# A two-layer decoder step: two small transfers change their queues, and the decode queries are spread in one step instead of two

## The chip, the cores and the metric

The kernel runs on one core of a Trainium2 chip. A core has TensorE (PE in the rows; PEld is its weight load), VectorE (DVE), ScalarE (ACT), GpSimd (POOL) and SyncE (SP), each with its own in-order stream of instructions, and 16 DMA engines that serve the queues on which SP, ACT and POOL issue transfers. The metric is the device time of one execution in microseconds (us).

## The reference

One inference step of a two-layer decoder for two groups with shared weights: a prompt of 512 tokens, and 8 samples of 8 new tokens each, which have 1024 tokens of past (576 token columns in all, model width 1024, float32). In short:

```
h = rmsnorm(x, norm1);  q, k, v, u, ga, gb = split(h @ w_in)        # 12 heads of 64
q, k = rope(q), rope(k)                                             # first 16 of 64 features
for (w, d) in ((128, 1), (512, 4), (2048, 16)):                     # 4 heads each
    query t attends keys t, t-d, t-2d, ... (w // d + 1 of them), in prompt or cache + new
o_a = the three groups' outputs mixed by softmax of their log-sum-exps
o_b = (mean of the last 2, 4, 8, 16 rows of u, minus u) @ pool_lin * pool_scale
x  = x + (sigmoid(ga) * (o_a @ w_pa) + sigmoid(gb) * (o_b @ w_pb)) @ w_o
x  = x + square(relu(rmsnorm(x, norm2) @ w_up)) @ w_down
outputs: final rmsnorm of x, the updated key/value windows of prompt and samples,
         the last 15 rows of u of the prompt (poolp) and of each sample (pools)
```

## The kernel before

Activations are kept transposed: features on partitions, the 576 tokens along the row. Every large product is done in three matmuls (high parts, and each low part with the other's high part); each weight tile is loaded by SP into `raw` or `rawu`, its high part is cast by ACT (`wh`) and its low part made by DVE (`wl`).

A layer goes through these stages. First q, k, v: for two head pairs p = 0, 1, units "d", "a", "b", "e", "c" (`qkv`, e for p = 0 alone), in which tokens stand on partitions; `unit_out` scales the result into `nat` (ACT; two buffers) and the samples' part into `DN`. While these run, the prompt's attention (`prompt(p)`) and the samples' attention (`decode(p, qb)`) of pairs 0 and 1 are woven in. Then the four `u` products of the pooling branch (`u_out`, `windows`, `lin`), the gate products with `w_pb` and `w_pa`, the `w_o` product, and the MLP, in which the sample caches are copied to the outputs from POOL's queue.

The order is written out at build time. PE's stream drives a clock `now`; generators ("sides") are resumed when that clock, a lane's modelled time or a marked event allows it. `Lane` and `Matrix` (lines 329 to 384) are models of the engines, and `transfer` (line 362) is that of a DMA: when the issuing engine has issued it and when it will have landed. They decide only where an instruction stands in its engine's stream; on the chip semaphores decide when it runs.

What the change touches:

- `turn(p, nat)`: values of unit c are needed with token 4n + r on partition n. `nat` (512 KB) is written to `DV` in HBM and read back as `vc` in that order, both on SP. `prompt(p)` uses `vc` in the matmuls into `O`. The `out_p` stores of `unit_out` read the same `nat`, also from SP.
- When pair 1's scores are done, the pool that holds `nat` is closed, and the tiles `u0` to `u3` are allocated in its memory (`pool_open`), so the first write to `u` waits for whoever still reads `nat`.
- `decode_q(p, DN)`: the 64 rows of queries (8 samples b, 8 tokens t, 384 numbers each) must stand in `qb` as 128 partitions (b, g), g = 0 to 15, each with all 8 tokens of its sample. They are stored to `DQ` (96 KB), spread to `DR` in HBM (1536 KB, 16 copies per sample), and loaded as `qb`. Pair 1 waits for event "K" of pair 0 ahead of the load, since `qb` has one buffer. `decode` multiplies cached keys (`kc`, four buffers, loaded by SP) with `qb` on DVE and POOL.
- `windows(sn)`: the last rows of u are transposed into PSUM (`pot`, one buffer), copied to `pn` by ACT, and stored: one store for `poolp`, eight for `pools`. `pn` is a tile of tag "t" with three buffers, which the gates' tiles (`tb`) and others use too. `lin` takes its PSUM from the same buffer as `pot`.

Of the kernel before, what the change touches and what calls it, by code (L numbers as in the profile page):

```python
# [7 lines left out]
F32 = mybir.dt.float32  # L8
# [9 lines left out]
NT, NP = 576, 512  # L18
NK = D // 128
UL = 15 + NP + 8 * 23  # L20
# [71 lines left out]
def hybrid_decoder_kernel(ctx: ExitStack, tc: tile.TileContext, a, o):  # L92
    nc = tc.nc
    T, V, S, G, Q = nc.tensor, nc.vector, nc.scalar, nc.gpsimd, nc.sync
# [4 lines left out]
    tp = ctx.enter_context(tc.tile_pool(name="tmp", bufs=3))  # L99
# [5 lines left out]
    drp = ctx.enter_context(tc.tile_pool(name="dr", bufs=1, space=DRAM))  # L105
# [12 lines left out]
    def v3(v, n):  # L118
        return v.rearrange("p (n d) -> p n d", n=n)
# [124 lines left out]
    def side(gen, delay=0.0):  # L244
        sides.append([now[0] + delay if not isinstance(delay, tuple) else delay, gen])

    def mark(*key, lat=0.0):
        ev[key] = now[0] + lat
# [27 lines left out]
    def place(x):  # L276

        t = x.tensor
        key = seen.get(t.name)
        if key is None:  # L280
            k = (t.slot_key, t.tag) if getattr(t, "slot_key", None) is not None else (t.name, None)
            n = count[k] = count.get(k, -1) + 1
            key = seen[t.name] = (k, n % (getattr(t, "bufs", None) or 1))
            old = slots.get(key)
            slots[key] = [max([old[0]] + [e[4] for e in old[1] + old[2]]) if old else 0.0, [], []]
        (step, n), *rest = x.ap
        p0, lo = divmod(x.offset, step) if step else (0, x.offset)
        return key, (p0, p0 + n, lo, lo + sum((c - 1) * abs(d) for d, c in rest) + 1)
# [4 lines left out]
    def hits(es, a, me):  # L293
        return [e[4] + (0.0 if e[5] is me else 0.1) for e in es
                if e[0] < a[1] and a[0] < e[1] and e[2] < a[3] and a[2] < e[3]]

    def due(outs, ins, me):
        t = 0.0
        for x in ins:
            key, a = place(x)  # L300
            t = max([t] + hits(slots[key][1], a, me))
        for x in outs:
            key, a = place(x)
            t = max([t, slots[key][0]] + hits(slots[key][1], a, me) + hits(slots[key][2], a, me))
        return t

    def note(outs, ins, end, me):
        for xs_, w in ((outs, 1), (ins, 2)):
            for x in xs_:
                key, a = place(x)  # L310
                es = slots[key][w]
                es[:] = [e for e in es if not (a[0] <= e[0] and e[1] <= a[1] and a[2] <= e[2] and e[3] <= a[3]
                                               and e[4] <= end)][-60:]
                es.append((*a, end, me))
# [8 lines left out]
    def size(x):  # L323
        n = 1
        for d in x.shape[1:]:
            n *= d
        return n
# [32 lines left out]
    wire, port = [0.0], [0.0]  # L360

    def transfer(lane, outs, ins):
        lane.t = max(lane.t, due(outs, ins, None)) + (0.5 if lane is G else 0.06)
        n = 4e-3 * outs[0].shape[0] * size(outs[0])
        wire[0] = max(wire[0], lane.t) + n / 270.0
        note(outs, ins, wire[0] + 1.9, wire)

    class Matrix:
# [26 lines left out]
    def ready(*aps, lag=0.2):  # L395
        return "at", max(now[0], due([], aps, None)) + lag
# [3 lines left out]
    S = Lane(S, 0.19, 1190.0)  # L400
    G = Lane(G, 0.12, 440.0)
    Q = Lane(Q, 0.0, 1.0)
# [102 lines left out]
    def rope(x, cos, sin, P, n, h):  # L505
        c16 = cos.unsqueeze(2).to_broadcast([P, n, h, 16])
        s16 = sin.unsqueeze(2).to_broadcast([P, n, h, 16])
        ta = tp.tile([128, 2, 256], F32, tag="t", name="rope")
        A = ta[:P, 0, :n * h * 16].rearrange("p (n h d) -> p n h d", n=n, h=h)
        B = ta[:P, 1, :n * h * 16].rearrange("p (n h d) -> p n h d", n=n, h=h)  # L510
        x16 = x[:, :, :, 0:16]
        V.tensor_mul(A, x16, c16)
        V.tensor_mul(B, x16, s16)
        V.tensor_add(x[:, :, :, 0:8], A[:, :, :, 0:8], B[:, :, :, 8:16])
        V.tensor_add(x[:, :, :, 8:16], A[:, :, :, 8:16], B[:, :, :, 0:8])
# [30 lines left out]
    for l in range(L):  # L546
# [80 lines left out]
        oa, tts, dns, vcs = [None, None], [{}, {}], [None, None], [None, None]  # L627
# [95 lines left out]

        def turn(p, nat):
            DV = drp.tile([512, 256], F32, tag=f"dv{l}{p}", name="DV")
            Q.dma_start(DV.rearrange("(j p) f -> p j f", j=4), nat)
            yield 2.8
            if p:
                yield ("O", 0)
            vcs[p] = pp.tile([128, 4, 256], F32, tag="vc", name="vc", bufs=1)  # L730
            Q.dma_start(vcs[p], DV.rearrange("(n r) f -> n r f", r=4))
            mark("V", "c", p, lat=3.0)

        def prompt(p):
# [127 lines left out]
        def decode_q(p, DN):  # L862
            rope(DN[:, 0:6].rearrange("p n (h d) -> p (n h) d", h=2).unsqueeze(1), *rope_d, 64, 1, 12)
            yield 1.6
            DQ = drp.tile([64, 384], F32, tag=f"dq{l}{p}", name="DQ")
            Q.dma_start(DQ, DN[:, 0:3].rearrange("p n f -> p (n f)"))
            yield 2.6
            DR = drp.tile([128, 3072], F32, tag=f"dr{l}{p}", name="DR")
            Q.dma_start(DR.rearrange("(b g) e -> b g e", b=8),
                        DQ.rearrange("(b t) e -> b (t e)", b=8).unsqueeze(1).to_broadcast([8, 16, 3072]))  # L870
            yield 3.6
            if p == 1:
                yield ("K", 0)
            qb = dp.tile([128, 8, 3, 128], F32, tag="qb", name="qb", bufs=1)
            Q.dma_start(qb.rearrange("p t n f -> p (t n f)"), DR)
            side(decode(p, qb))

        def decode_new(p, DN):
# [188 lines left out]
        up = bp = None  # L1067
# [19 lines left out]
        def windows(sn):  # L1087
            yield 3.0
            yield ready(sn, lag=1.0)
            ptr = trp.tile([128, 512], F32, tag="tr", name="trs")  # L1090
            for g in range(4):
                T.transpose(ptr[:, 120 * g:120 * g + 120], sn[:, 128 * g:128 * g + 128], ident[0:120, 0:120])
            for g in range(4):
                S.copy(v3(U[g][:, 15 + NP:], 8)[:, :, 0:15], v3(ptr[:, 120 * g:120 * g + 120], 8))
            for g in (3, 2, 1, 0):
                yield ("u", g, l)
                cur = U[g]
                for d in range(g + 1):
                    w = 1 << d
                    nx = up.tile([128, UL], F32, tag="s", name="s", bufs=2)  # L1100
                    s0 = 2 * w - 1
                    V.tensor_add(nx[:, s0:], cur[:, s0:], cur[:, s0 - w:UL - w])
                    cur = nx
                    yield after(V, lag=0.0)
                V.tensor_mul(cur[:, 15:31], cur[:, 15:31], cnt[:, g])
                if g == 0:
                    yield ("ob", 3, l)
                pg = up.tile([128, NT], F32, tag="pg", name="pg", bufs=3)
                sc = 1.0 / (2 << g)
                V.scalar_tensor_tensor(out=pg[:, 0:NP], in0=cur[:, 15:15 + NP], scalar=sc, in1=U[g][:, 15:15 + NP],  # L1110
                                       op0=ALU.mult, op1=ALU.subtract)
                V.scalar_tensor_tensor(out=v3(pg[:, NP:], 8), in0=v3(cur[:, 15 + NP:], 8)[:, :, 15:23], scalar=sc,
                                       in1=v3(U[g][:, 15 + NP:], 8)[:, :, 15:23], op0=ALU.mult, op1=ALU.subtract)
                pgs[g] = pg
                mark("pg", g, l, lat=max(V.t - now[0], 0.0))
                yield after(V, lag=0.0)
            for n in range(2):
                pot = trp.tile([128, 512], F32, tag="tr", name="trp")
                m = 15 if n == 0 else 64
                for g in range(4):  # L1120
                    src = U[g][:, NP:NP + 15] if n == 0 else ud[:, g]
                    T.transpose(pot[0:m, 128 * g:128 * g + 128], src, ident)
                pn = tp.tile([128, NT], F32, tag="t", name="pn")
                S.copy(pn[0:m, 0:512], pot[0:m, :])
                if n == 0:
                    Q.dma_start(o["poolp"][l], pn[0:15, 0:512])
                else:
                    for b in range(8):
                        Q.dma_start(o["pools"][l, b, 7:15], pn[8 * b:8 * b + 8, 0:512])
                yield 1.0  # L1130
            mark("w", l)

# [73 lines left out]
        for f in range(8):  # L1206
# [9 lines left out]
            t = gate.pop(0)  # L1216
# [411 lines left out]
```

## Time and profile before

| | us |
|---|---|
| median of 3 runs | 1762.05 (1757.75 to 1764.63) |
| profiled execution | 1757.92 |
| its span, first to last instruction | 1756.2 |
| PE busy | 1632.0 |
| DVE busy | 1158.4 |
| ACT busy | 695.4 |
| POOL busy | 229.7 |
| mean granted clock of TensorE | 0.962 of full speed |

The DMA engines moved 255.21 MB, a mean of 145 GB/s; SP's queue carried 198.46 MB of it. An engine that is idle costs time only where PE, the busiest, waits for it in turn. The rows of the trace are read with that question: at which places does PE stand, and what ends its wait.

### The profile page before, as it was taken

The numbers are of one execution on the slowest core, as the hardware profiler recorded it, in microseconds if no ns is written. First come the engines' busy times: TensorE is split into PE (matmuls) and PEld (weight loads), VectorE is DVE, ScalarE is ACT, GpSimd is POOL, SyncE is SP. The second block draws the span as 40 slices with busy tenths as digits, with TensorE's granted clock in tenths as the row PEclk, the third lists the DMA queues.
The fourth block names the chain that finished last, engine by engine and source line by source line (L and its number), as shares of the span: only waits on it lengthen the run. The fifth ranks groups of instructions, "written<-read, shape, count | busy, mean of one in ns | idle before, by whom it ended". The sixth has DMA issues, their size and how long they took to land.

```text
span 1756.2 us, 30640 instructions
## 1 busy us (share of the span) xinstructions
PE 1632.0 (93%) x12608; PEld 1585.7 (90%) x12608; DVE 1158.4 (66%) x1892; ACT 695.4 (40%) x1210; POOL 229.7 (13%) x350
## 2 busy tenths in 40 slices
PE   8989778899989999999999889798998999999995
PEld 8989768889889999999999878697997999999995
DVE  5589468745766666666736865884566776666763
ACT  6545232123444433344445433221344433344443
POOL 0041013000011111121001400230000211111202
PEclk9999889989989999999999999898998999999998
DMA  4564543434235545552427364325251445554521
GB/s 172 182 191 151 176 124 108 135 97 134 101 114 190 184 163 179 191 174 86 138 77 253 118 220 148 112 88 141 88 189 44 173 169 172 191 177 162 180 64 54
DMA packets 140005, 255.21 MB, mean 145 GB/s; under 512 B 9660, under 2 KB 100284, under 8 KB 137034
## 3 DMA queue, kind: packets, MB, share of 16 engines
q1 hardware_dynamic: 135498, 198.46, 35.4%
q0 software_dynamic: 3648, 53.98, 8.5%
q8 instruction: 99, 1.62, 0.4%
q10 hardware_dynamic: 720, 0.82, 0.1%
q14 instruction: 40, 0.33, 0.1%
HBM read 239.40 MB, written 74.87 MB: 179 GB/s over the span
## 4 chain that ended last, share of the span: by engine, by line
PE 78%; DVE 9%; DMA 6%; ACT 4%; issue 2%; SPq 1%; POOL 1%; POOLq 0%; DVEq 0%; ACTq 0%
PE mm L380 42%; PE mmq L380 10%; PE pa L380 10%; PE pc L380 5%; PE pb L380 2%; DVE wl L357 2%; DMA DV<-nat 2%; PE po L380 2%; PE psd L380 2%; DMA kc<-in_c 1%; ACT wh L357 1%; SPq L340 1%; PE sp L380 1%; PE O L380 1%; DVE SC L357 1%
## 5 line engine op out<-in xcount | busy, mean ns | idle before, releaser
L380 PE MATMUL mm<-m,wh 128*128 128x256 f32 (+1 forms) x2560 | 451.6, 297 | 3.4 <-DVE xr L357 2.1
L380 PEld LDWEIGHTS mm<-m,wh 128*128 128x128 f32 x2560 | 387.6, 190 | 4.4 <-ACT wh L357 1.7
L380 PE MATMUL mm<-m,wl 128*128 128x320 f32 (+1 forms) x1280 | 282.3, 298 | 7.2 <-DVE wl L357 7.2
L357 DVE TENSOR_TENSOR wl<-raw,wh 128x1024 fp32r<-128x1024 f32 (+2 forms) x195 | 218.5, 1122 | 83.4 <-ACT wh L357 80.1
L357 ACT CAST wh<-rawu 128x512 fp32r<-128x512 f32 (+1 forms) x158 | 123.1, 783 | 351.5 <-DVE rawu L357 299.9
L380 PE MATMUL mm<-a,wh 128*128 128x256 f32 (+1 forms) x1280 | 233.9, 306 | 22.4 <-DVE ud L357 17.0
L357 ACT CAST wh<-raw 128x1024 fp32r<-128x1024 f32 (+2 forms) x195 | 183.1, 940 | 151.6 <-PE mm L380 97.8
L380 PEld LDWEIGHTS mm<-m,wl 128*128 128x128 f32 x1280 | 218.3, 190 | 8.2 <-DVE wl L357 8.2
L380 PEld LDWEIGHTS mm<-a,wh 128*128 128x128 f32 x1280 | 196.8, 195 | 27.0 <-issue 26.0
L380 PE MATMUL mmq<-wh,a 128*128 128x256 f32 x1152 | 215.8, 288 | 1.6 <-ACT a L357 0.7
L357 DVE TENSOR_TENSOR xr<-xr,mm 128x576 f32<-128x576 f32 (+2 forms) x152 | 108.8, 716 | 116.3 <-PE mm L380 111.9
L380 PEld LDWEIGHTS mmq<-wh,a 128*128 128x128 f32 x1152 | 179.7, 192 | 4.3 <-issue 1.4
L357 DVE TENSOR_TENSOR wl<-rawu,wh 128x512 fp32r<-128x512 f32 (+1 forms) x158 | 140.2, 889 | 64.8 <-ACT wh L357 62.1
L380 PE MATMUL pa<-h,wh 128*128 128x288 f32 x896 | 181.6, 295 | 0.0
L357 POOL COPY pace<-beat 1x1 f32<-1x1 f32 x112 | 61.2, 547 | 863.1 <-DVE beat L357 863.1
L380 PE MATMUL mmq<-wl,a 128*128 128x256 f32 x576 | 163.4, 284 | 0.0
L380 PEld LDWEIGHTS pa<-h,wh 128*128 128x128 f32 x896 | 144.9, 188 | 0.0
L380 PE MATMUL mm<-a,wl 128*128 128x256 f32 (+1 forms) x640 | 139.7, 301 | 0.0
L380 PE MATMUL pa<-h,wl 128*128 128x288 f32 x448 | 132.3, 295 | 0.0
L380 PEld LDWEIGHTS mm<-a,wl 128*128 128x128 f32 x640 | 110.8, 194 | 0.0
L380 PEld LDWEIGHTS mmq<-wl,a 128*128 128x128 f32 x576 | 110.4, 192 | 0.0
L380 PE MATMUL pc<-h,wh 128*128 128x288 f32 x512 | 104.5, 295 | 0.0
(210 smaller groups left out, 2547.1 us busy)
## 6 DMA issues: line engine op xcount, KB each, us to landing
out_s<-in_c POOLq DMA_DIRECT2D x64, 508.0 KB, 5.1
rawu<-in_wup SPq DMA_DIRECT2D x60, 512.0 KB
raw<-in_wd SPq DMA_DIRECT2D x60, 512.0 KB
kc<-in_c SPq DMA_DIRECT2D x40, 512.0 KB
raw<-in_wq SPq DMA_DIRECT2D x35, 512.0 KB
kc<-in_c SPq DMA_DIRECT2D x64, 256.0 KB
out_s<-in_c POOLq DMA_DIRECT2D x32, 504.0 KB, 5.1
raw<-in_wgb SPq DMA_DIRECT2D x16, 512.0 KB
```

Source lines behind the costliest of these rows:

```text
L340: return op(*args, **kw)
L357: return op(*args, **kw)
L380: return self.eng.matmul(out, w, x, **kw)
```

## The change

Values' round trip: the store to `DV` goes from SP's queue to ACT's, the load of `vc` to POOL's. The query spread: `DR` is left out; eight loads on SP, one for each sample, take the 12 KB of the sample's rows in `DQ` sixteen times, into the 16 partitions of `qb` that belong to it. Pooled rows: `pn` is now a tile of tag "s" of the pool of `u` (two buffers, those of the window sums), the `poolp` store is issued by ACT and the eight `pools` stores by POOL. The planner's model of a DMA is changed: an SP transfer takes SP's modelled time at 240 GB/s, ACT's issue costs 0.1, and all share a wire of 300 GB/s that no longer starts from the moment of issue.

```diff
@@ def transfer(lane, outs, ins)
-        lane.t = max(lane.t, due(outs, ins, None)) + (0.5 if lane is G else 0.06)
         n = 4e-3 * outs[0].shape[0] * size(outs[0])
-        wire[0] = max(wire[0], lane.t) + n / 270.0
+        lane.t = max(lane.t, due(outs, ins, None)) + (n / 240.0 if lane is Q else 0.5 if lane is G else 0.1)
+        wire[0] = max(wire[0] + n / 300.0, lane.t)
         note(outs, ins, wire[0] + 1.9, wire)
@@ def turn(p, nat)
-            Q.dma_start(DV.rearrange("(j p) f -> p j f", j=4), nat)
+            S.dma_start(DV.rearrange("(j p) f -> p j f", j=4), nat)
@@
-            Q.dma_start(vcs[p], DV.rearrange("(n r) f -> n r f", r=4))
+            G.dma_start(vcs[p], DV.rearrange("(n r) f -> n r f", r=4))
@@ def decode_q(p, DN)
             yield 2.6
-            DR = drp.tile([128, 3072], F32, tag=f"dr{l}{p}", name="DR")
-            Q.dma_start(DR.rearrange("(b g) e -> b g e", b=8),
-                        DQ.rearrange("(b t) e -> b (t e)", b=8).unsqueeze(1).to_broadcast([8, 16, 3072]))
-            yield 3.6
             if p == 1:
                 yield ("K", 0)
             qb = dp.tile([128, 8, 3, 128], F32, tag="qb", name="qb", bufs=1)
-            Q.dma_start(qb.rearrange("p t n f -> p (t n f)"), DR)
+            for b in range(8):
+                Q.dma_start(qb[16 * b:16 * b + 16].rearrange("p t n f -> p (t n f)"),
+                            DQ[8 * b:8 * b + 8].rearrange("t e -> (t e)").unsqueeze(0).to_broadcast([16, 3072]))
@@ def windows(sn)
-                pn = tp.tile([128, NT], F32, tag="t", name="pn")
+                pn = up.tile([128, UL], F32, tag="s", name="pn", bufs=2)
                 S.copy(pn[0:m, 0:512], pot[0:m, :])
                 if n == 0:
-                    Q.dma_start(o["poolp"][l], pn[0:15, 0:512])
+                    S.dma_start(o["poolp"][l], pn[0:15, 0:512])
                 else:
                     for b in range(8):
-                        Q.dma_start(o["pools"][l, b, 7:15], pn[8 * b:8 * b + 8, 0:512])
+                        G.dma_start(o["pools"][l, b, 7:15], pn[8 * b:8 * b + 8, 0:512])
```

## Rows read from the trace of the kernel before

**Rows 1.** The page: busy us and share of the span of each engine, instructions.

```profile
PE 1632.0 (93%) x12608; PEld 1585.7 (90%) x12608; DVE 1158.4 (66%) x1892; ACT 695.4 (40%) x1210; POOL 229.7 (13%) x350
```

**Rows 2.** By stretches: length, busy PE, PEld, DVE, ACT, POOL; clock, DMA share, GB/s.

```profile
240.00:260.00 20.00, 9.37 (x56) 7.86 (x54) 15.05 (x23) 5.92 (x13) 5.84 (x6) 0.76 0.39 113
```

**Rows 3.** Chain of waits in order of time: start, us, what; the three places.

```profile
96.13 6.34 DMA DV<-nat
102.48 4.84 DMA vc<-DV
...
177.29 9.53 DMA DV<-nat
...
187.87 4.66 PE mm L380 x18
...
249.20 3.00 DMA out_poolp<-pn
...
963.40 6.01 DMA vc<-DV
...
1037.75 10.09 DMA DV<-nat
```

**Rows 4.** Waits by name at the three places: total us, times, longest.

```profile
PE O L380 <- DMA vc<-DV: 3.0, 1, 3.0
PE O L380 <- DMA vc<-DV: 3.5, 1, 3.5
DVE u L357 <- DMA DV<-nat: 11.7, 1, 11.7
ACT pn L357 <- DMA out_poolp<-pn: 6.8, 1, 6.8
```

**Rows 5.** ACT in order of time: start, us; unit c of both pairs.

```profile
87.62 1.57 ACT L357 ACTIVATE nat<-mmq,rs 128x256 f32<-128x256 f32 x4 [2.06 <-PE mmq L380]
...
160.58 1.57 ACT L357 ACTIVATE nat<-mmq,rs 128x256 f32<-128x256 f32 x4 [4.23 <-PE mmq L380]
```

**Rows 6.** SP's queue in order of time: start, us of issue, what.

```profile
63.94 0.80 SPq L340 DMA_DIRECT2D DR<-DQ  x1
74.06 0.34 SPq L340 DMA_DIRECT2D qb<-DR  x1
...
161.36 6.37 SPq L340 DMA_DIRECT2D kc<-in_c  x1
...
1024.04 9.48 SPq L340 DMA_DIRECT2D kc<-in_c  x5
```

**Rows 7.** By stretches, as rows 2, around the places.

```profile
178.00:188.00 10.00, 0.90 (x7) 0.70 (x5) 1.07 (x4) 0.12 (x1) 0.24 (x4) 0.71 0.65 225
188.00:194.00 6.00, 6.00 (x33) 6.00 (x34) 4.11 (x8) 2.26 (x4) 0.00 (x0) 0.63 0.60 209
...
1039.00:1049.00 10.00, 2.09 (x16) 1.89 (x15) 1.01 (x4) 0.07 (x1) 0.24 (x4) 0.84 0.78 254
...
340.00:362.00 22.00, 14.35 (x173) 10.55 (x172) 7.84 (x28) 0.82 (x3) 0.00 (x0) 0.71 0.49 137
...
64.00:74.00 10.00, 10.00 (x89) 9.40 (x88) 7.40 (x15) 7.13 (x23) 0.00 (x0) 1.00 0.43 168
...
172.00:185.00 13.00, 6.77 (x50) 6.53 (x50) 3.17 (x5) 3.40 (x14) 0.00 (x0) 0.89 0.96 311
```

**Rows 8.** DVE in order of time, with the idle time before and its end.

```profile
88.50 1.22 DVE L357 TENSOR_TENSOR prod<-kc,qb 128x1024 f32<-128x1024 f32 x1
...
246.43 2.17 DVE L357 SCALAR_TENSOR_TENSOR pg<-s,u 128x512 f32<-128x512 f32 x2
...
254.80 0.48 DVE L357 SCALAR_TENSOR_TENSOR ob<-lp,gains,ob 128x256 fp32r<-128x256 f32 x1 [3.21 <-ACT ob L357]
```

**Rows 9.** DMA issues by tile: shortest, median, longest ns, first and last start.

```profile
L340 POOL DMA_DIRECT2D out_s<-in_c x112: 486/486/534, 504.2 to 1665.4; - x112
L340 SPq DMA_DIRECT2D DV<-nat x4: 832/1392/2602, 96.1 to 1037.7; - x4
```

## The prediction

> **What bounds the kernel now.** The first table of the page is read first: TensorE (PE) is busy for 1632.0 of 1756.2 us, VectorE (DVE) for 66%, ScalarE (ACT) for 40%, POOL for 13% [rows 1]. So 124 us of the span are without a matmul, and only these, and the stretches at the lower clock behind them, can be won. The table by stretches is read next, for where they lie, as 10.6 of the 20 us at 240 to 260 [rows 2]; then the chain of waits, for what ends them [rows 3], and the waits by name [rows 4]. Three places of each layer belong to this change.
>
> *(a)* Unit c of head pair 0: `DV` is issued at 96.13 and has landed 6.34 us later, `vc` takes 4.84 from issue to landing (6.01 in layer 1), and PE stands 3.0 us for it (3.5 in layer 1) [rows 3, 4].
>
> *(b)* Unit c of pair 1: ACT has finished `nat` at 160.58 + 1.57 = 162.15 [rows 5], but SP issues `DV` only at 177.29, behind five `kc` loads, `qb`, two `out_p` stores and a weight load. It lands at 177.29 + 9.53 = 186.8 [rows 3]; the `u` tiles take the memory of `nat`, so DVE waits 11.7 us [rows 4], and PE, 0.90 us busy in 178 to 188 with 0.13 of it after the restart at 187.87, stands from 178.77 on: 9.1 us. In layer 1 `DV` lands at 1037.75 + 10.09 = 1047.8, and PE stands for the 7.9 us that it is not busy in 1039 to 1049 [rows 3, 7].
>
> *(c)* The second `pn` copy waits 6.8 us for the store of the first [rows 4], because both came to the same buffer; that store is issued only at 249.20 and lands 3.00 us later [rows 3], behind `kc` loads that wait for their own buffers. `lin`'s matmuls wait for the PSUM that this copy reads.
>
> The clock follows: behind place (b) the stretch 188 to 194 runs at a mean of 0.63, between 2.4 GHz (1.00) and 1.2 (0.50) [rows 7].
>
> **The change, part by part.**
>
> *(a), the round trip on ACT and POOL.* `nat` of pair 0 is ready at 87.62 + 1.57 = 89.2 [rows 5], so `DV` can start 7 us earlier. With the longest legs of the rows, 6.34 + 6.01, `vc` is there by 102, and PE stands from about 104.4 (the landing at 107.3 less 3.0) [rows 3, 4]. So 3.0 + 3.5 us go. What is late next is DVE, which has the products of the decoding to do meanwhile; for that I count 6.0 for both layers.
>
> *(b), the same at pair 1.* Without `DV`, the two `out_p` stores of the same `nat` stay on SP behind the loads of `qb`: the wait for `DV` becomes one for `out_p`. When do these land? The write of `DR` is gone, and with it the full queue in which one `kc` load took 6.37 us to issue [rows 6]. From that issue, 161.36, five `kc` loads (2 MB) at the 311 GB/s of 172 to 185 [rows 7] end 6.6 us later, at 167.9; then come the eight loads of `qb`, X us; 0.5 MB of `out_p`, 1.7; and 2 to land, an estimate from the legs of rows 3 less their bytes. That is 171.6 + X against 186.8 now. PE restarted 1.0 after the landing and stood from 178.77, so nothing is left of the stall up to X = 6.1, and nothing is won from X = 15.2 on.
>
> X has no row: no load of 16 partitions stands in the trace. From below, `qb<-DR`, the same bytes into the same tile, moves among the traffic of 172 to 185: 1.57 MB at 311 GB/s, 5.1 us. From the side of the source, `DR<-DQ`, as many bytes spread from the same rows, had landed when SP issued `qb` at 74.06: 9.3 us after its own issue was over at 63.94 + 0.80 [rows 6]. From above, 16 partitions are an eighth of 128: at 311/8 GB/s, 41 us. I take 9.3, the nearest row with this source. Then `out_p` lands at 180.9 and PE stands 3.2 instead of 9.1 us: 5.9 won, plus the slow stretch, 0.37 of 6 us, 2.2 [rows 7]. Layer 1: 1024.04 + 6.6 + 9.3 + 3.7 = 1043.6 against 1047.8: 4.2, and as more idling is left there, half of that 2.2 [rows 3, 6, 7]. Together 13.4.
>
> While `DR` is written the DMA engines are busy for a share of 0.43, in 172 to 185 for 0.96 [rows 7]. The Trainium skill (DMA: Bandwidth & Descriptors, Rules for kernel authors) says that a leading dimension below 16 keeps a DMA on that many engines; `DR` has 8 in front, the new loads 16. By that rule X would be near 5.1, not 9.3. The same skill (SBUF — State Buffer, Door 1: The DMA port swizzle) speaks against the change: 16 partitions reach only 4 of 16 ports, with 104 GB/s measured there. By it, as an estimate, 1.57 MB take 15 us and (b) wins almost nothing; no row here shows it.
>
> *(c), `pn`.* The tile moves to a tag with two buffers of its own, so the second copy needs the one that the last window sum leaves once `pg` has read it: at 246.43 + 2.17 = 248.60 [rows 8], where the store landed at 252.2 [rows 3]: 3.6 us earlier. DVE stands 3.21 us ahead of `ob` there [rows 8] and is the next limit, 15.05 of 20 us busy [rows 2]. So 3.2 for each layer, 6.4.
>
> *What is added.* ACT issues four `DV` and two `poolp`, 0.83 to 2.6 us each by SP's rows for `DV` [rows 9]; ACT's idle time (5.92 of 20 us busy at (c) [rows 2]) covers them, and without that cover PE would wait at most as long as the issue of `kc` once took, 6.4. POOL issues four `vc` and sixteen `pools` at 486 ns by the nearest row [rows 9], 10 us in all, beside the products of the decoding; POOL has 5.84 of 20 us busy at (c) [rows 2]. `vc` also waits on POOL for `DV` to land; behind it stand POOL's products, and DVE's folds wait for those, one step later. I count 4 us lost, between 0 and the 10. SP issues 32 short loads and loses 36 transfers: nothing.
>
> *The order.* The planner's prices change (SP at 240 GB/s in order, a wire of 300), and `qb` needs a step less: 8 x 0.82 + 1.9 = 8.5 instead of 2 x (5.8 + 1.9) = 15.4 us by its own numbers, so it places pair 0's decoding some 7 us earlier. This moves instructions on all engines; I can't price it, and keep 8 us either way.
>
> Sum: 6.0 + 13.4 + 6.4 - 4 = 22 us off the profiled execution's 1757.92: 1736. That execution is 4.1 below the median of the runs, 1762.05; against the median, as all times below, 1740.
>
> **The rivals.** A change below 0.5% (8.8 us) can't be told from none here.
>
> *Narrow loads take back (b).* X is 15 to 16 us: `out_p` lands where `DV` did. For it: SP's ring is served in order, and `DR` shows that these bytes need not move at the full rate. Against: `DR` itself was faster. Left are 6.0 + 6.4 - 4 = 8.4 us: 1754. It is what the port rule would do. 0.20.
>
> *Slower: the narrow loads choke SP's ring.* Same place, larger X; it decides where (a) and (c) are eaten up too, 8.4/2 = 4.2 us beyond 15.2, X above about 19. At X = 30 `out_p` lands 14.8 us later than `DV` did, and pair 0's first product, at 88.50 now [rows 8], waits for 63.94 + 30 + 1.6 (its `kc`) = 95.5, 7.0 us; both twice, less 8.4: 1797. For it speaks only the bound from above; against it the two nearer ones. 0.08.
>
> *The gain is given back.* PE stops again in 340 to 362, for 7.7 us [rows 7], where the gates with `w_pa` need the end of pair 1's decoding. If that chain doesn't move up with PE, (a) to (c) only lengthen this wait. Against: PE, DVE and ACT run static orders, so the decoding's steps move up with what stands ahead of them. About 1760. 0.12.
>
> *More.* X is 5.1 and the earlier decoding shortens the wait at 340: (b) is 9.1 + 7.9 + 2 x 2.2 = 21.4, the total 30, and up to twice 7.7 on top: 1732 down to 1717. 0.18.
>
> My forecast keeps 0.42.
>
> **How the numbers follow.** Faster by over 0.5% (under 1753): nearly all of the forecast and of "more", half of the first rival, a little of the third, 0.70. Within 0.5%: the rest of the first, most of the third, 0.20. Slower: 0.10. The range takes in "more" and, above, the first and third rival with the order's 8 us: 1714 to 1768; the slower rival and the tails are left out. The likeliest case's own range is 1728 to 1754 (POOL between 0 and 10, the order 8 either way).
>
> **What would show it.** (a) PE's wait for `vc` is gone. (b) DVE's wait ahead of the first `u` is below 6 us and ended by `out_p`; the loads of `qb` are over within 10 us of the first. If they take 15 or more, the port rival holds. (c) The second `pn` copy comes within 4 us of the first. The decoding's first product stands at about 82. I am wrong if the first `u` still waits 9 us or more, if POOL's products trail DVE's by a whole step, or if the wait at 340 grows by what was won ahead of it.

## The result, and the profile after

The changed kernel takes 1743.76 us (median of 4 runs, 1738.51 to 1745.91), the kernel before 1760.99 beside it (1757.75 to 1764.63): a ratio of 0.9897, 95% interval 0.9867 to 0.9928. 1740 was predicted, inside a range of 1714 to 1768. The total was right, by luck, since its parts were not: the runs below show that place (a) gave nothing, that PE's stops at (b) shrank by less than half of what was put down for them, and that what (c) gave came not from the wait named, but for the most part from the end of the kernel, which the prediction doesn't mention.

The profiled execution took 1745.91 us, span 1744.1 against 1756.2. Its page, by engine (as [rows 1]):

```profile
PE 1638.9 (94%) x12608; PEld 1592.0 (91%) x12608; DVE 1166.7 (67%) x1892; ACT 695.4 (40%) x1210; POOL 239.6 (14%) x370
```

The chain of waits at the first two places and in layer 1 (start, us, what; as [rows 3]):

```profile
62.53 4.13 DMA DQ<-dn
67.06 5.73 DMA qb<-DQ
72.80 7.87 DMA kc<-in_c
...
173.46 10.34 DMA DV<-nat
184.25 3.12 DMA out_p<-nat
188.47 7.92 PE mm L380 x42
...
1030.77 10.87 DMA DV<-nat
1041.65 0.40 SPq L340
1042.10 3.13 DMA out_p<-nat
```

`vc` has left the chain, and with it PE's wait for it. At place (b) `DV` is still there, and `out_p`, which SP issued ahead of `DV` before (173.64 against 177.29), now comes after it in the chain. The waits by name, layer 0 (total us, times, longest; as [rows 4]):

```profile
SPq L340 <- DMA DV<-nat: 5.8, 1, 5.8
DVE u L357 <- DMA out_p<-nat: 8.5, 1, 8.5
PE mm L380 <- DVE ud L357: 5.9, 1, 5.9
PE lq L380 <- ACT pn L357: 2.0, 1, 2.0
```

PE's stop at (b) is 5.9 us where it was 9.1; in layer 1 the same row says 6.4 where it was 7.9. PE comes out of it at 188.47 in layer 0, 0.6 us later than before (187.87), and at 1046.32 in layer 1, 2.6 us earlier (1048.92). The second `pn` copy no longer waits for a store, and PE's wait ahead of `lq` is 2.0 instead of 6.7 us. SP in order of time (start, us of issue, what; as [rows 6]):

```profile
159.95 7.36 SPq L340 DMA_DIRECT2D kc<-in_c  x5
167.40 9.38 SPq L340 DMA_DIRECT2D qb<-DQ  x8
177.66 0.36 SPq L340 DMA_DIRECT2D raw<-in_wgb  x1
183.81 0.95 SPq L340 DMA_DIRECT2D out_p<-nat  x2
```

SP is free at 178.0 and issues `out_p` only at 183.81, in the moment in which `DV` has landed (173.46 + 10.34). And ACT in order of time shows why `DV` starts so late:

```profile
165.87 1.53 ACT L357 ACTIVATE nat<-mmq,rs 128x256 f32<-128x256 f32 x4
...
173.40 0.51 ACT L357 ACTIVATE SC<-SC 128x368 f32<-128x368 f32 x1 [2.45 <-DVE SC L357]
173.46 0.37 ACTq L340 DMA_DIRECT2D DV<-nat  x1
```

`nat` is ready at 167.40, but in ACT's own program `DV` stands behind a scaling, a cast of weights, four exponentials of `P` and one that waits 2.45 us for DVE: 6.1 us. At pair 0, place (a), the round trip comes no earlier than before (ACT, POOL, PE):

```profile
94.88 1.57 ACT L357 ACTIVATE nat<-mmq,rs 128x256 f32<-128x256 f32 x4
96.72 0.38 ACTq L340 DMA_DIRECT2D DV<-nat  x1
...
103.26 0.73 POOL L340 DMA_DIRECT2D vc<-DV  x1
...
112.69 0.61 PE L380 MATMUL O<-PT,vc 128*64 128x128 f32 x8
```

`nat` is ready at 96.45 instead of 89.2, `DV` goes out at 96.72 (96.13 before), and `vc`, 4.0 us from issue to landing, is there at 107.3 as before; but PE comes to it at 112.69 where it was 107.37. The rate of the narrow loads shows by stretches (length, busy PE, PEld, DVE, ACT, POOL; clock, DMA share, GB/s):

```profile
72.00:74.00 2.00, 2.00 (x19) 1.82 (x20) 0.87 (x2) 1.68 (x7) 0.00 (x0) 1.00 1.18 141
74.00:76.00 2.00, 2.00 (x23) 1.88 (x20) 1.47 (x3) 1.98 (x7) 0.00 (x0) 1.00 0.82 98
82.00:84.00 2.00, 2.00 (x19) 2.00 (x18) 0.31 (x2) 0.19 (x2) 0.00 (x0) 1.00 1.16 290
...
173.00:175.00 2.00, 2.00 (x17) 1.81 (x17) 0.89 (x3) 1.60 (x6) 0.00 (x0) 1.00 0.92 151
177.00:179.00 2.00, 2.00 (x18) 2.00 (x17) 1.96 (x4) 1.30 (x5) 0.00 (x0) 1.00 1.11 351
```

The DMA engines are about as busy while `qb` comes in as afterwards, and move a third to a half as much. Pair 0's loads are issued from 66.68 on and the rate is back at 82: X is 15 us; for pair 1, 167.40 to 177, 10 us. (The Trainium skill, SBUF — State Buffer, Door 1: The DMA port swizzle, gives 104 GB/s for a target of 16 partitions; pair 0's 98 to 104 GB/s from 74 to 80 agree, pair 1's 151 to 153 from 173 to 177 lie above it.)

Last, the end. PE's last matmul ends at 1743.4 before and at 1737.9 after: only 5.5 us of the profiled pair's 12.0 lie ahead of it. The rest goes with one instruction, POOL's DRAIN, which ends the program behind the last operation (shortest, median, longest ns, first and last start; first the kernel before, then the changed one):

```profile
L1617 POOLq DRAIN  x3: 34/102/11521, 1743.9 to 1755.9; - x3
```

```profile
L1615 POOLq DRAIN  x3: 40/93/3277, 1738.3 to 1743.9; - x3
```

It took 11.52 us and takes 3.28, part of it beside POOL's last operation; the kernel ended 12.8 us after PE and ends 6.3 us after it.

### The profile page after: what moved, and what is told of

It is laid out like the page before. It is cut to its first block, busy times and chain, and to the rows that moved or that the text cites. A ratio compares the mean times of both kernels' runs of the same rounds, so it can differ in the third digit from the quotient of the medians.

```text
span 1744.1 us, 30710 instructions
## 1 busy us (share of the span) xinstructions
PE 1638.9 (94%) x12608; PEld 1592.0 (91%) x12608; DVE 1166.7 (67%) x1892; ACT 695.4 (40%) x1210; POOL 239.6 (14%) x370
## 4 chain that ended last, share of the span: by engine, by line
PE 76%; DVE 10%; DMA 6%; ACT 4%; issue 2%; SPq 0%; POOL 0%; DVEq 0%; POOLq 0%; ACTq 0%
PE mm L380 41%; PE pa L380 10%; PE mmq L380 10%; PE pc L380 5%; DMA kc<-in_c 2%; PE pb L380 2%; DVE wl L357 2%; PE po L380 2%; PE psd L380 2%; DMA DV<-nat 1%; ACT wh L357 1%; PE O L380 1%; DVE SC L357 1%; PE trx L384 1%; DVE xr L357 1%
```

## The experiments

Each ratio is to the kernel before, run beside it on the same chip (medians 1761.58 for e1 to e4, 1762.28 for e5 to e8, 1762.71 for e9 to e12).

**e1: the eight loads to all partitions.**

```diff
-for b in range(8):
-    Q.dma_start(qb[16 * b:16 * b + 16]..., DQ[8 * b:8 * b + 8]....to_broadcast([16, 3072]))
+for t in range(8):
+    Q.dma_start(qb[:, t]..., DQ.rearrange("(b t) e -> b t e", b=8)[:, t].unsqueeze(1).to_broadcast([8, 16, 384]))
```

> The queries are spread by eight loads as in the changed kernel (same source rows, same 1.57 MB, same queue), but each load writes one of the eight tokens to all 128 partitions in place of all tokens to 16 partitions. Theory 'narrow target' (a load into 16 partitions moves about 112 GB/s; the 14 us of pair 0 are the target's): all eight are over within 7 us of the first issue, the first decode product comes 5 to 7 us earlier than 85.9, out_p of pair 1 lands near 180 in place of 187.4, and the time is 4 to 8 us below the changed kernel, about 1736 to 1740. Rival 'source' (the same 96 KB of rows are read sixteen times over, and that is slow however it is written; the old spread of the same rows took 9.3 us): the loads still take 9 to 14 us and the time stays within 3 us of the changed kernel's 1743.8.

1729.25 us, 0.9814 (0.9792 to 0.9836): more than either forecast. Pair 1's loads, by stretches:

```profile
163.00:165.00 2.00, 2.00 (x19) 1.88 (x18) 1.77 (x3) 1.95 (x6) 0.00 (x0) 1.00 1.17 295
165.00:167.00 2.00, 2.00 (x20) 1.67 (x19) 1.97 (x5) 2.00 (x6) 0.00 (x0) 1.00 0.99 262
167.00:169.00 2.00, 2.00 (x15) 1.81 (x15) 2.00 (x5) 0.69 (x4) 0.00 (x0) 1.00 0.59 167
169.00:171.00 2.00, 2.00 (x18) 2.00 (x17) 1.63 (x5) 0.51 (x1) 0.00 (x0) 1.00 0.54 184
```

262 to 295 GB/s at first, with `kc` loads that were issued just before still among them; then 167 and 184 at shares of 0.59 and 0.54, where the narrow ones had 151 and 153 at about 0.9. So the narrow target kept the DMA engines busier for less, but the wide loads by themselves are not much faster: SP hands them over in 7.7 us instead of 9.4. (The pieces shrink with the shape, from 12 KB to 1.5 KB; no run separates the two.) Pair 0 is like it: from 66 to 74 the DMA share is 0.33 to 0.60 with 115 to 169 GB/s, SP is done with `qb` and the five `kc` loads after 15.5 us, against 17.0 in the changed kernel, and the first product comes at 82.76, 3.1 us earlier, not 5 to 7. (A share of about half would suit the rule of the Trainium skill, DMA: Bandwidth & Descriptors, Rules for kernel authors, on a leading dimension of 8; no run here settles it.) Most comes from place (b):

```profile
162.39 7.71 SPq L340 DMA_DIRECT2D qb<-DQ  x8
170.19 0.40 SPq L340 DMA_DIRECT2D raw<-in_wgb  x1
170.64 0.98 SPq L340 DMA_DIRECT2D out_p<-nat  x2
```

`out_p` goes out ahead of `DV` (171.87 on ACT) and beside it, and has landed at 180.7; DVE's wait for it is 5.2 us and PE's stop 2.6, in layer 1 3.8.

**e2: one load from the rows.**

```diff
-(eight loads)
+Q.dma_start(qb..., DQ.rearrange("(b t) e -> b (t e)", b=8).unsqueeze(1).to_broadcast([8, 16, 3072]))
```

> As e1, but one load of 1.57 MB into all 128 partitions, straight from the rows with the spread in its source. If the eight DMA semaphores, which SP's and ACT's transfers take in turn, are what holds the kc loads and out_p behind the queries (each waits until the transfer that last had its semaphore has landed), SP issues the five kc loads behind this one load without a wait of over 2 us, whatever the load itself takes, and out_p waits only for DV's semaphore; then 1733 to 1738. If only the bytes matter (theory 'narrow target'), it stands with e1 to within 2 us. If eight rows in front of the source keep a load on eight DMA engines, it takes 9 us or more and the time is that of the changed kernel or up to 6 us above it.

1753.01 us, 0.9951 (0.9935 to 0.9966), slower than all three forecasts. With a single transfer ahead of them, the five `kc` loads took SP longer than in any other run:

```profile
66.17 0.73 SPq L340 DMA_DIRECT2D qb<-DQ  x1
66.95 19.38 SPq L340 DMA_DIRECT2D kc<-in_c  x5
```

The issue of the third load alone took 12.67 us, and SP waited for nothing else in these 19 us. So it isn't the eight semaphores that hold these `kc` loads, but the slow transfer in the queue ahead of them; and the shape of the load decides (eight loads of 196 KB, one per token, against one of 1.57 MB).

**e3: the old spread of the queries.**

```diff
+DR = drp.tile([128, 3072], ...); Q.dma_start(DR..., DQ....to_broadcast([8, 16, 3072])); yield 3.6
-(eight loads)
+Q.dma_start(qb..., DR)
```

> The changed kernel with the old spread of the queries: one write to 128 rows in DRAM, one load of them; the values' round trip and the pooled rows stay on ACT and POOL. Theory 'narrow target': the narrow loads are worth little against the old way (14 us from the first load against about 15 from the write's issue to the landing of the load in the kernel before), so the time is 1738 to 1748 and nearly all of the gain of 17 us is there without them. Rival 'the direct spread is the gain' (the prediction's place b, 13.4 us): 1753 to 1758.

1753.89 us, 0.9959 (0.9943 to 0.9974): 10 us of the gain go, the rival's figure. PE's stop at (b) is 7.2 us. Even narrow, the direct spread is worth this much.

**e4: the values' round trip back on SP.**

```diff
-S.dma_start(DV..., nat)
+Q.dma_start(DV..., nat)
-G.dma_start(vcs[p], DV...)
+Q.dma_start(vcs[p], DV...)
```

> The changed kernel with DV and vc back on SP's queue in their old order; pooled rows on ACT and POOL and the eight loads stay. By the prediction's place (a), PE waits for vc of pair 0 again and 6.0 us are lost; behind the narrow loads, DV of pair 1 comes still later than before, so that (b) is lost too: 1752 to 1764. Rival: the order that the planner writes now puts PE's use of vc so late (112.5 in place of 107) that it no longer waits for it, and only pair 1 loses: 1745 to 1750.

1739.68 us, 0.9873 (0.9855 to 0.9891). Nothing is lost, and both forecasts failed; the interval overlaps that of the changed kernel, and in the profiled executions PE ends 6.9 us earlier (1731.0). PE waits 1.3 us for `vc` of pair 0, but its stop at (b) is gone in both layers:

```profile
153.33 5.33 SPq L340 DMA_DIRECT2D kc<-in_c  x5
158.71 3.06 SPq L340 DMA_DIRECT2D out_p<-nat  x2
161.87 3.97 SPq L340 DMA_DIRECT2D qb<-DQ  x8
...
172.09 0.98 SPq L340 DMA_DIRECT2D out_p<-nat  x2
173.12 0.70 SPq L340 DMA_DIRECT2D DV<-nat  x1
179.19 0.34 SPq L340 DMA_DIRECT2D vc<-DV  x1
```

On SP `DV` is issued no later than on ACT (173.12 against 173.46) and lands after 6.1 us instead of 10.3; here the planner has the `kc` loads, and so `qb`, out 6 us earlier, and `out_p` stands ahead of `DV`.

**e5: the pooled rows' part undone.**

```diff
-pn = up.tile([128, UL], F32, tag="s", name="pn", bufs=2)
+pn = tp.tile([128, NT], F32, tag="t", name="pn")
-S.dma_start(o["poolp"]...); G.dma_start(o["pools"]...)
+Q.dma_start(o["poolp"]...); Q.dma_start(o["pools"]...)
```

> The changed kernel with the pooled rows' part undone: pn takes the old shared buffer and its nine stores go back to SP; the rest stays. By the prediction's place (c) PE waits 3.2 us more for each layer's second pn copy: 6.4 us lost, 1750. Rival: with the new order of the planner DVE's ob is the limit there (PE already waits 2.4 us for ob ahead of trp in the changed kernel), so no more than 2 us are lost: 1742 to 1746. Either way the last DRAIN of POOL is read: 11.5 us in the kernel before, 3.0 to 3.3 in the five runs whose pools are on POOL; if these sixteen stores are the reason, it is above 9 again here and another 6 us are lost.

1753.95 us, 0.9953 (0.9939 to 0.9967): 10 us lost, but not where the prediction had them. With the shared buffer and the stores back on SP the second `pn` copy still waits for no store, and PE's wait ahead of `lq` is 2.0 us as in the changed kernel; so it was the rest of the change that ended this wait, not `pn`'s buffer (in e8, the spread alone, it is 1.0):

```profile
248.97 0.58 ACT L357 COPY pn<-trp 64x512 f32<-64x512 f32 x1 [2.73 <-PE trp L384]
```

PE's last matmul ends at 1737.8, as in the changed kernel (1737.9), and the end is long again:

```profile
L1615 POOLq DRAIN  x3: 40/102/11854, 1738.2 to 1750.6; - x3
```

**e6: the planner's prices alone**, `transfer` of the changed kernel in the kernel before.

> The kernel before with the planner's new transfer prices alone; no queue is changed. The prediction kept 8 us either way for the order. Theory 'the order matters little, the gain is the direct spread's and the end's': 1757 to 1765. Rival 'the order is most of the gain' (the run with the values' round trip back on SP was 4 us faster than the changed kernel, so the queues by themselves are not what it lives from): 1745 to 1752. The last DRAIN of POOL stays above 9 us if it hangs on POOL's stores, and falls to about 3 if it hangs on the order.

1765.17 us, 1.0016 (1.0002 to 1.0030), DRAIN 11.5. The order by itself gains nothing.

**e7: e1 and e4 together.**

> Two steps together that each beat the changed kernel: the eight spread loads written to all 128 partitions (1729.25), and the values' round trip back on SP in the planner's order (1739.68). If both act at the same place (the landing of DV and out_p ahead of the first u of pair 1), they don't add up: 1726 to 1731. If they act at different places, 14.5 + 4 us: 1724 to 1726. If SP's queue becomes the limit with DV behind the spread: 1732 to 1738.

1736.24 us, 0.9856 (0.9832 to 0.9880), 7 us above e1, the third of the three cases. The two steps don't add up, and each way of spreading the queries has its own best place for the values; that SP's queue is the limit with wide loads is not shown by a trace.

**e8: the narrow spread alone**, the old prices, queues and `pn`.

> The kernel before with one edit: the write of DR and its load give way to the eight narrow loads; prices, values' round trip and pooled rows stay as before. Undoing the same edit in the changed kernel cost 10 us (1753.89 against 1743.76). Theory 'the narrow loads are worth something by themselves, as they save the write of DR and its landing': 1748 to 1754. Rival 'they only pay with the round trip off SP or with the new order': 1757 to 1765, with DV of pair 1 landing at 185 or later.

1745.46 us, 0.9909 (0.9876 to 0.9941), below the theory's 1748: nearly the whole change in one edit, though its runs lie far apart (1736.63 to 1757.87). The end is as long as before (DRAIN 11.5), so all of it is gained ahead of PE's last matmul. `DV` is on SP here, behind eight narrow loads:

```profile
152.78 5.12 SPq L340 DMA_DIRECT2D kc<-in_c  x5
157.95 2.58 SPq L340 DMA_DIRECT2D out_p<-nat  x2
160.62 4.83 SPq L340 DMA_DIRECT2D qb<-DQ  x8
...
172.54 0.58 SPq L340 DMA_DIRECT2D DV<-nat  x1
```

```profile
DVE u L357 <- DMA DV<-nat: 3.5, 1, 3.5
```

Without the write of `DR` and the wait for it the `kc` loads start 8 us earlier than before (152.78 against 160.72) and take 5.12 us to issue, and `DV` lands at 181.2 instead of 186.8. This is what the prediction said of place (b), except that `DV` needn't leave SP for it.

**e9: the stores of the pooled rows of the samples on POOL**, nothing else.

```diff
-Q.dma_start(o["pools"][l, b, 7:15], pn[...])
+G.dma_start(o["pools"][l, b, 7:15], pn[...])
```

> The kernel before with one edit: the sixteen stores of the pooled rows of the samples go to POOL; pn's buffer, poolp, the values and the spread stay. Theory 'the end': POOL's last DRAIN ends 9.4 to 9.7 us after POOL's last operation in all four kernels that have 114 or 118 transfers on POOL, and 0.8 to 1.2 us after it in all six that have 130 or 134; here there are 130, so the DRAIN is over within 1.5 us, and the time falls by 6 to 9 us, to 1753 to 1756, with PE's last matmul within 3 us of that of before. Rival 'the end hangs on the shared buffer or on poolp': the DRAIN stays above 9 us after the last operation and the time stays at 1759 to 1764.

1747.30 us, 0.9913 (0.9899 to 0.9928), 6 us below the forecast.

```profile
L1617 POOLq DRAIN  x3: 34/93/2951, 1741.3 to 1747.1; - x3
```

The DRAIN is over 0.8 us after POOL's last operation (9.4 before): these sixteen transfers on POOL's queue are the reason, neither `pn`'s buffer nor `poolp`. The profiled pair shows 6.2 us at the end and 2.6 ahead of it; the planner also puts `tb` earlier on DVE between 270 and 290 here, and PE waits 2.0 us for it instead of 4.7. The medians differ by 15.4; some 6 us of that stand in neither trace and stay open (the profiled execution of the kernel before, 1757.92, lies 4.8 below the median of this round, that of e9 is the slowest of its four).

**e10: forty idle instructions on POOL.**

```diff
+for _ in range(40):
+    G.memset(pace, 0.0)
```

> The kernel before with forty more instructions at the start of POOL's program, which clear eight floats each and which nobody waits for; 114 transfers on POOL, as before. It tells apart what the last DRAIN hangs on. Theory 'number of transfers that POOL issues': still 9.4 us after the last operation, 1759 to 1764. Rival 'length of POOL's program' (in the trace POOL has 559 to 581 rows where the DRAIN is long, 584 to 598 where it is short): about 600 rows here, so the DRAIN is over within 1.5 us and the time is 1753 to 1756.

1762.24 us, 1.0000 (0.9981 to 1.0019).

```profile
L1619 POOLq DRAIN  x3: 34/102/11519, 1746.9 to 1759.0; - x3
```

599 rows on POOL and the same 9.4 us: not the length of its program.

**e11: wide loads and `pn`'s part, old prices, values on SP.**

> The kernel before, old prices and the values' round trip on SP, with the eight loads to all 128 partitions and with pn's part of the change. If the parts add up: 1762, less 17 for the direct spread (e8), less 8.5 for the end of POOL (pnback less the changed kernel was 10), less what wide loads give over narrow ones, 0 to 14: 1722 to 1737. It differs from e7 in the prices alone, 1736.24 there. Theory 'the new prices cost 3 us' (e6): 1731 to 1735. Rival 'with wide loads it is the round trip on SP that holds, whatever the order' (e7 was 7 us above e1): 1736 to 1742.

1736.34 us, 0.9851 (0.9837 to 0.9866): the rival's case. It is level with e7, so the prices make no difference here; e1 differs from e7 by the values' way alone, and with wide loads ACT and POOL are the better way, by 7 us. With narrow loads (e4) they were not.

**e12: e1 with `DV` and unit c's `out_p` on POOL.**

```diff
-S.dma_start(DV..., nat)
+G.dma_start(DV..., nat)
-Q.dma_start(o["p" + n]..., nat...)
+(G if unit == "c" else Q).dma_start(o["p" + n]..., nat...)
```

> e1, the fastest so far (1729.25), with DV and the two out_p stores of unit c issued by POOL in place of ACT and SP. In e1 ACT finishes nat some 4 us before DV's issue, since DV stands behind exponentials in ACT's program, and DVE still waits 5.2 us ahead of the first u of pair 1 for DV and out_p; POOL does nothing there. Theory 'DV's issue is what is late': u's wait falls below 2 us, 2 to 4 us less in each layer: 1722 to 1727. Rival 'the DMA engines are full there (share 0.74 to 1.13 in 160 to 175), so an earlier issue lands no earlier': 1728 to 1731. Against: for pair 0 the same three issues stand behind POOL's products of the decoding, at up to 2.4 us each, and vc comes later: up to 1735.

1733.10 us, 0.9832 (0.9818 to 0.9847): no better than e1. DVE's wait ahead of the first `u` and PE's stop there are gone, as the theory had it, but pair 0 pays for it, as the objection said:

```profile
PE O L380 <- DMA vc<-DV: 4.2, 1, 4.2
```

e1 stays the fastest: 1729.25 us, 14.5 below the changed kernel.

## Why the prediction was right in total and wrong in its parts

*(a), 6.0 us forecast: nothing, or a loss.* The wait for `vc` is gone, but not by the way forecast: in layer 0 `vc` landed at 107.3 as before, and PE came to it 5.3 us later; in layer 1 it was issued at 960.57 (963.40 before), and PE came to it at 970.00, 0.5 us later than after its wait before (969.46). The decoding's first product came at 85.89, not at 82, since pair 0's narrow loads took 15 us; PE then stood 2.5 us for what follows on DVE, and the last matmul of layer 0's `mmq` starts 3.8 us later than before (164.1 against 160.3; 2.7 of these are there by 38 us, ahead of every changed transfer). These 2.7 are the granted clock of this one execution: behind the same stop of PE, 2.5 us long and over at 29.92, it is 1.00 (2.4 GHz) in the profile before and 0.50 (1.2 GHz) in the one after, from 31 to 34 us:

```profile
31.00:34.00 3.00, 3.00 (x28) 3.00 (x27) 1.29 (x2) 1.05 (x1) 0.00 (x0) 1.00 0.02 5
```

```profile
31.00:34.00 3.00, 3.00 (x16) 3.00 (x16) 1.17 (x2) 1.04 (x1) 0.00 (x0) 0.50 0.00 0
```

By e4 the move of the round trip gained nothing in company of the narrow loads. What failed is "with the longest legs of the rows ... `vc` is there by 102": it took `nat` to be ready at 89.2 as before, but in the new order it was ready at 96.45, behind the first steps of the decoding, for which PE stood. The price was put on the wait alone, not on what the same queue was given in its place.

*(b), 13.4 us forecast, 10.1 of it for PE's stops: 4.7.* The two stops shrank by 3.2 and 1.5 us, not by 5.9 and 4.2; in layer 0 PE came to its stop 3.8 us late, so that nothing was won there. DVE's wait ahead of the first `u` is 8.5 us and in layer 1 9.1, not below 6; 9 was the prediction's own sign of being wrong. X, taken at 9.3, was 15 for pair 0 and 10 for pair 1. The issue of the `kc` loads was right (167.3 against 167.9), and so was the end of `qb` for pair 1, 177 against 177.2. The step that failed stands behind that: "the wait for `DV` becomes one for `out_p`", landing at 171.6 + X. It landed at 187.4, 6.2 us after that sum with the measured X (9.6), for two reasons. `DV` sits in ACT's program 6.1 us behind `nat`. And SP may not issue `out_p` until `DV` has landed, though they share no data to wait for: in the built program SP's and ACT's transfers take eight completion semaphores in turn, `out_p` is the eighth behind `DV` in both layers and waits for its semaphore, and the trace has SP waiting 5.8 us for it (8.3 in layer 1). So a transfer moved off SP's queue still held SP's queue. In e1 and e4, where `out_p` goes out first, that wait isn't there; no run changes the semaphores alone.

*The direct spread* was priced only through (b). By e8 alone it gives 16.8 us, by e3 10 of the changed kernel's: with `DR`'s write and landing gone, `kc`, `qb` and `DV` of pair 1 all move forward in e8, and both layers gain. The parts don't add up: alone the spread gives 16.8 us and the `pools` stores (e9) 15.4, the whole change 17.2. The rival that by the port rule gave 1754 had the rate right for pair 0 and the result wrong: slow loads of 10 to 15 us still replace a write, a wait and a load that took longer together.

*(c), 6.4 us forecast: 6.5 at the end, a coincidence, as the reason was wrong.* The two copies came 5.0 us apart (247.73 and 252.76; 7.4 before, forecast within 4), and PE's wait ahead of `lq` fell, but by e5 the rest of the change did that, and new waits for `ob` (2.4 us) and `pa` (1.8) took its place. PE ends where it ends without this part (e5), but e5's profile doesn't have the 2.7 us lost by 38; PE's wait for `tb` behind the pooling is 1.5 us and 1.6 in layer 1 with this part, 3.4 and 3.8 without. So a few us ahead of PE's last matmul are likely, though not shown by themselves. The 6.5 us are POOL's final DRAIN.

*Cost on POOL and ACT, 4 us:* not seen as such; the issues are short (0.38 us for `DV` on ACT, 0.50 for `pools` on POOL). SP gave up 34 transfers and not 36 (502 issues before, 500 after); nothing hung on that. *Order, 8 either way:* e6 puts it at +2.9 by itself, e11 against e7 at nothing. *The gain given back* at 340 to 362: not seen; between 333 and 364 PE waits 7.6 us in all where it was 7.5, in layer 1, between 1195 and 1224, 8.7 where it was 8.6.

Ahead of PE's last matmul 5.5 us were won where 22 were forecast, and 6.5 at the end where none were; the median moved 17.2, 5 more than the profiled pair, which has the slowest of the changed kernel's four runs. The 2.7 us that it lost to the clock by 38 us may be part of those 5; the rest stands in neither trace.

## What to carry to other kernels

A transfer that moves to another queue takes its place in that engine's program and, if the queues share semaphores, keeps its hold on the old queue: ask what stands ahead of it in the new program, and which transfer behind it on the old one is due on the same semaphore. A wait that has gone is no gain by itself: its data may have come earlier, or the engine later. Try a load across all partitions, in several transfers of middle size (here eight of 196 KB beat one of 1.57 MB by 24 us), before asking from which queue. And read the trace behind the last matmul too: an end that waits for an idle engine is time like any other.

## What the runs showed of the hardware

- POOL's last DRAIN goes by the number of transfers on POOL's queue. It ends 9.40 us after POOL's last operation in the kernels with 114 of them, 9.73 with 118, 0.82 with 130, 1.15 with 134 and 2.14 with 146 (14 kernels; those with the same number agree within 0.01 us). On either side of the drop each further transfer adds 82 to 83 ns, be it four `vc` (e5, and 130 to 134) or `DV` and `out_p` (e12); so it isn't these stores by themselves. By that slope, as an estimate, 9.40 us are 114 transfers and 0.82 are 10: as if 120 no longer counted. No run has between 119 and 129, and why the count falls back isn't shown.
- The same 1.57 MB from the same 64 rows: narrow, eight loads of 16 partitions, 98 to 153 GB/s at a DMA share of 0.8 to 1.2 (70 to 80 and 173 to 177 us); wide, eight loads of 128 partitions, 115 to 184 GB/s at a share of 0.33 to 0.60; one wide load was slowest, 20 us for SP to hand over it and five `kc` loads.
- The granted clock behind the same stop of PE differs from one execution to the next: at 31 to 34 us it is 1.00 before and in e5, 0.50 in the changed kernel, 0.56 in e3 and 0.62 in e1.
